# Input laid by groups of tokens, squares added up on VectorE and GpSimd, and a tied order of the first operands, at the head of a one-layer decoder step

## The chip, the core and the metric

The kernel runs on one core of one Trainium2 chip. The metric is the device time of one execution in microseconds (us). The engines are TensorE (PE, its weight loads PEld), VectorE (DVE), ScalarE (ACT), GpSimd (POOL) and SyncE (SP), from whose queue all transfers are issued.

## What is computed

One layer of a hybrid decoder for 1024 prompt tokens and 8 sample tokens, with a model width of 1024. What the change touches is only its first step, the norm and the start of the one wide projection behind it:

```
def _rmsnorm(x, g):
    y = xf * lax.rsqrt(jnp.mean(xf * xf, axis=-1, keepdims=True) + RMS_EPS)
    return (y * g.astype(F32)).astype(x.dtype)
...
xn = _rmsnorm(x, p['norm_mix_g'])
proj = xn @ p['w_in']
pr, pm, pg = ...   # columns for RWKV-7 time mixing, for mLSTM, and for two gates
y_r = RWKV7(pr); y_m = mLSTM(pm)
x = x + (sigmoid(g_r) * (y_r @ r_up) + sigmoid(g_m) * (y_m @ m_up)) @ w_out
x = x + relu(_rmsnorm(x) @ ffn_w1)^2 @ ffn_w2
```

All is in float32.

## The kernel before

**Layout.** The width of 1024 lies in eight slices (k = 0 to 7) of 128 partitions, the tokens lie along the columns. There are 1032 tokens and 8 columns more for the shifted state, in three groups g of 344, 344 and 352 columns (344 of them for the norm). `load_x(g)` loads the eight slices of one group, one transfer each.

**The norm.** `x_rstd(g)` squares the eight slices on ACT (`sq`), and adds them up over slices and partitions with eight float32 matmuls of a matrix of ones into one PSUM bank (`psb`). ACT makes the root's inverse of it with an Ln and an Exp (`rsx`). `x_norm(g)` then works slice by slice: a *mul* on DVE (the gain and `rsx` times `x`, in place), a *hi* on ACT (`xh`, the value rounded to PE's fast float32 format), and a *lo* on DVE (`xl`, what the rounding left).

**The projection.** A weight tile of 128 columns is loaded raw and split in the same way into `whi` (ACT) and `wlo` (DVE). A product takes three matmuls for each slice: `whi` with `xh`, `whi` with `xl`, `wlo` with `xh`. The first two weight tiles (`first_w`) run group by group as soon as operands are there, tile after tile within a group, into banks `psm`. All later tiles run all three groups in turn. 48 matmuls, 24 to a tile, are a token group's work for the first two tiles. `x_last`, the norm of the third group, is called by `emit_jobs` after the first group's products. An evacuation of a product is an ACT copy (`m`) and a DVE instruction that reads the bank (`lw` and `sxg` for the first two tiles).

**What sets the order.** Instructions are recorded one after the other and a scheduler then chooses the order on each engine by its own estimates; each engine works strictly in that order. `tc.issue_after(ins)` ties what is recorded in it behind an instruction. All transfers go through SP's queue in order. Buffers are shared by tags: `v`, `rk`, `ar`, `bk` and `bkt` are later used by the RWKV stage.

**Warming.** `warm(n)` runs n float32 products of `ones` with itself, which nobody reads.

Of the kernel before, what the change touches and what calls it, by code (L numbers as in the profile page):

```python
# [86 lines left out]
def hybrid_step(ctx: ExitStack, tc: tile.TileContext, I: dict, O: dict):  # L87
    nc = tc.nc
    V, S, G, PE = nc.vector, nc.scalar, nc.gpsimd, nc.tensor
    dma = nc.sync.dma_start  # L90
# [3 lines left out]
    wp = ctx.enter_context(tc.tile_pool(name="wp", bufs=2))  # L94
# [7 lines left out]
    ones = cp.tile([128, 128], F32, name="ones")  # L102
    par = cp.tile([128, NPAR], F32, name="par")
    bias = cp.tile([128, 8], F32, name="bias")
    par2 = cp.tile([128, 18], F32, name="par2")
    xo = cp.tile([128, KD, 9], F32, name="xo")
# [18 lines left out]
    def P(name, i=0, rows=slice(0, 128)):  # L125
        c0 = PCOLS[name] + i
        return par[rows, c0 : c0 + 1]
# [7 lines left out]
    def mm(out, lhsT, rhs, start, stop):  # L135
        return PE.matmul(out, lhsT, rhs, start=start, stop=stop)  # L136

    def tt(out, a, b, op):
        V.tensor_tensor(out, a, b, op)  # L139

    def stt(out, a, s, b, op0, op1):
        V.scalar_tensor_tensor(out, a, s, b, op0, op1)  # L142

    def act(out, in_, f, **kw):
        return S.activation(out, in_, f, **kw)  # L145
# [9 lines left out]
    MUL, ADD, SUB, MAX, MIN = ALU.mult, ALU.add, ALU.subtract, ALU.max, ALU.min  # L155
# [7 lines left out]
    def bb():  # L163
        return bank("b", "psb", 3)
# [10 lines left out]
    def gst(name, dt=F32):  # L175
        return gp.tile([128, 346], dt, name=name, tag="gst")

    dma(par[:], I["par"])
    G.memset(ones[:], 1.0)
    log_exp_set()  # L180
    for i, v in enumerate([RMS_EPS, R_GN_EPS, M_GN_EPS, 1.0, 10.0 * math.log(2.0)]):
# [1 line left out]
    B_RMS, B_RGN, B_MGN, B_ONE, B_KK = (bias[:, i : i + 1] for i in range(5))  # L183

    def warm(n):

        pt = bb()
        for i in range(n):
            mm(pt[:, 0:128], ones[:], ones[:], i == 0, i == n - 1)


    def wload(src):
        raw = wp.tile([128, KD, 128], F32, name="wraw", tag="wraw")
        dma(raw[:], src)
        return raw

    def wsplit(raw):
        hi = wp.tile([128, KD, 128], F32R, name="whi", tag="whi")
        lo = wp.tile([128, KD, 128], F32R, name="wlo", tag="wlo")
        act(hi[:], raw[:], AF.Copy)  # L200
        tt(lo[:], raw[:], hi[:].bitcast(F32), SUB)
        return hi, lo
# [32 lines left out]
    def R(shape, name, tag=None, bufs=1, dt=F32):  # L235
        return rp.tile(shape, dt, name=name, tag=tag or name, bufs=bufs)


    xr4 = R([128, 4, NX], "xr4", tag="v")
    xr = [xr4[:, k] for k in range(4)]  # L240
    for k in range(4, KD):
        xr.append(R([128, NX], f"xr{k}", tag=("ar", "bk")[k // 6], bufs=2)[:])

    def load_x(g):
        c0, c1 = RGROUPS[g]
        for k in range(KD):
            dma(xr[k][:, c0:c1], I["xT"][:, k, c0:c1])

    load_x(0)
    first_w = [wload(I["win"][i]) for i in (12, 13)]  # L250
    load_x(1)
    load_x(2)
    dma(con[:], I["con"])
    xa = []
    for k in range(KD):
        xh = xp.tile([128, NX], F32R, name=f"xh{k}", tag=f"x{2 * k}")
        xl = xp.tile([128, NX], F32R, name=f"xl{k}", tag=f"x{2 * k + 1}")
        xa.append((xh, xl))

    rsx = R([128, 3, GN], "rsx", tag="uv", bufs=2)  # L260

    def x_rstd(g):

        c0, c1 = GROUPS[g]
        rs = rsx[:, g]
        pt = bb()
        for k in range(KD):
            sq = gst("sq")[:, :GN]
            act(sq, xr[k][:, c0:c1], AF.Square)
            mm(pt[:, :GN], ones[:], sq, k == 0, k == KD - 1)  # L270
        if g == 0:
            warm(16)
        act(rs, pt[:, :GN], AF.Ln, scale=1.0 / D, bias=B_RMS)
        act(rs, rs, AF.Exp, scale=-0.5)
        dma(d_rs[0:1, c0:c1], rsx[0:1, g])

    def x_norm(g, ks=range(KD)):
        c0, c1 = GROUPS[g]
        for k in ks:
            xh, xl = xa[k]  # L280
            x = xr[k][:, c0:c1]
            stt(x, x, P("g1", k), rsx[:, g], MUL, MUL)
            c2 = RGROUPS[g][1]
            act(xh[:, c0:c2], xr[k][:, c0:c2], AF.Copy)
            tt(xl[:, c0:c2], xr[k][:, c0:c2], xh[:, c0:c2].bitcast(F32), SUB)

    x_rstd(0)
    first_w[0] = wsplit(first_w[0])
    x_norm(0, range(4))
    first_w[1] = wsplit(first_w[1])  # L290
    x_norm(0, range(4, KD))
    x_rstd(1)
    x_norm(1)
    x_rstd(2)

    def x_last():
        x_norm(2)
        for k in range(KD):
            G.tensor_copy(xo[:, k, :], xr[k][:, NT - 9 : NT])
        dma(O["xo"], xo[:])  # L300


# [4 lines left out]
    def evac_shift(dst, ti):  # L307

        mu, omu = P("mu", ti), par2[:, ti : ti + 1]
        carry = {}  # L310

        def f(g, pt):
            c0, c1 = RGROUPS[g]
            n = min(c1, NT) - c0
            m1 = carry.pop(g, None)
            if m1 is None:
                m1 = gst("m1")
                G.memset(m1[:, 0:1], 0.0)
            npr = min(c1, T) - c0
            act(m1[:, 1:npr + 1], pt[:, 0:npr], AF.Copy, scale=mu)  # L320
            if g < 2:
                nx = gst("m1")
                G.tensor_copy(nx[:, 0:1], m1[:, npr:npr + 1])
                carry[g + 1] = nx
            else:
                act(m1[:, npr : npr + NS], pt[:, NT - c0 : NX - c0], AF.Copy, scale=mu)
            stt(dst[:, c0 : c0 + n], pt[:, :n], omu, m1[:, 0:n], MUL, ADD)

        return f
# [125 lines left out]
    def prep(hp):  # L455
# [1199 lines left out]
    order = [0, 4, 1, 5, 2, 6, 3, 7]  # L1655
# [65 lines left out]
    for g, st in enumerate(STEPS):  # L1721
        n = len(st)
# [6 lines left out]
        for u in range(7 * n):  # L1729
            p, j = divmod(u, n)  # L1730
# [3 lines left out]
    n = len(STEPS[3])  # L1734
# [36 lines left out]
    parts = [(0, (0, 1)), (1, (0,)), (1, (1,))]  # L1771
# [144 lines left out]
```

## Time and profile before

| | |
|---|---|
| median of 3 runs | 1664.7 us (1663.85 to 1669.45) |
| the profiled execution | 1665.72 us, its span 1663.9 us |
| busy PE, PEld | 1615.5 us (97%), 1536.9 us (92%) |
| busy DVE, ACT, POOL | 1187.9 us (71%), 758.9 us (46%), 67.2 us (4%) |
| transfers | 200.11 MB, mean 120 GB/s |

The span is the time between the first and the last instruction; the execution's own time is 1.8 us longer. Busy PE is not PE at its peak: matmuls are pipelined, and a recorded matmul lasts longer than the distance to the next one. The speed is read from the distance of starts.

### The profile page before, as it was taken

Reading aid. Unit: us, or ns where it says so; the run is one execution under the profiler, and the core shown is the slowest. Engines: PE = TensorE matmul, PEld = TensorE weight load, DVE = VectorE, ACT = ScalarE, POOL = GpSimd, SP = SyncE. Lnnn points to the kernel's source line nnn. Section 1 sums busy time; section 2 is a strip of 40 time slices with the busy share of each in tenths; the row PEclk is TensorE's granted clock in tenths of the full one; section 3 lists DMA queues with packets and bytes.
Section 4 is the critical chain, followed back from the end, with each engine's and each line's share of the span. In section 5 each row is a group of like instructions: output and inputs, shape, how many; then the busy total and the mean of one; then the engine's idle time right before and its main releaser. Section 6 shows DMA issues by size and latency. Waiting matters only on the chain. (4 is left out here: it accounts for less than half of the span.)

```text
span 1663.9 us, 37007 instructions
## 1 busy us (share of the span) xinstructions
PE 1615.5 (97%) x15338; PEld 1536.9 (92%) x15338; DVE 1187.9 (71%) x2258; ACT 758.9 (46%) x1387; POOL 67.2 (4%) x130
## 2 busy tenths in 40 slices
PE   8999998999999998999999999999999899999997
PEld 7999986888888887899999999999999899999996
DVE  6266658665666597765876798777777787878787
ACT  6466653333332442443544664445555552525324
POOL 1000000000000000000000222000000000000001
PEclk9999999999999999999999999999999999999998
DMA  5133353222211333424743244444434562625212
GB/s 186 52 117 117 106 170 105 65 92 85 81 61 39 127 105 64 108 90 100 255 150 110 97 130 150 148 141 147 147 141 143 176 217 73 208 77 179 90 58 103
DMA packets 111687, 200.11 MB, mean 120 GB/s; under 512 B 18755, under 2 KB 49502, under 8 KB 111006
## 3 DMA queue, kind: packets, MB, share of 16 engines
q1 hardware_dynamic: 111518, 197.73, 37.1%
q8 instruction: 121, 1.98, 0.5%
q14 instruction: 48, 0.39, 0.1%
HBM read 139.73 MB, written 57.95 MB: 119 GB/s over the span
## 5 line engine op out<-in xcount | busy, mean ns | idle before, releaser
L136 PE MATMUL psm<-xh,whi 128*128 128x344 f32 (+2 forms) x1024 | 342.6, 335 | 0.4 <-DVE rkt L142 0.4
L136 PE MATMUL psm<-xh,wlo 128*128 128x344 f32 (+2 forms) x1024 | 332.0, 325 | 0.0
L136 PE MATMUL psm<-xl,whi 128*128 128x344 f32 (+2 forms) x1024 | 331.1, 324 | 0.0
L136 PE MATMUL bank<-hc,wc 128*128 128x258 f32 x2520 | 306.3, 283 | 9.8 <-ACT su L145 4.5
L136 PEld LDWEIGHTS bank<-hc,wc 128*128 128x128 f32 x2520 | 303.9, 190 | 12.2 <-ACT su L145 4.7
L136 PEld LDWEIGHTS psm<-xh,whi 128*128 128x128 f32 (+1 forms) x1024 | 191.5, 187 | 13.3 <-issue 7.7
L136 PEld LDWEIGHTS psm<-xl,whi 128*128 128x128 f32 (+1 forms) x1024 | 191.8, 188 | 4.2 <-issue 1.9
L136 PEld LDWEIGHTS psm<-xh,wlo 128*128 128x128 f32 (+1 forms) x1024 | 191.8, 187 | 2.1 <-issue 0.5
L136 PE MATMUL bank<-cmb,wc 128*128 128x258 f32 x1536 | 189.8, 282 | 0.8 <-ACT s L145 0.5
L136 PEld LDWEIGHTS bank<-cmb,wc 128*128 128x128 f32 x1536 | 186.1, 189 | 1.3 <-ACT s L145 0.7
L136 PE MATMUL bank<-ha,wc 128*128 128x258 f32 x1152 | 143.5, 282 | 0.7 <-DVE u L139 0.4
L136 PEld LDWEIGHTS bank<-ha,wc 128*128 128x128 f32 x1152 | 139.9, 189 | 1.1 <-DVE u L139 0.6
L139 DVE TENSOR_TENSOR wlo<-wraw,whi 128x1024 fp32r<-128x1024 f32 (+1 forms) x65 | 78.7, 1210 | 78.8 <-ACT whi L145 78.8
L145 ACT ACTIVATE wc<-wraw 128x512 fp32r<-128x512 f32 (+1 forms) x109 | 66.2, 612 | 114.6 <-PE bank L136 101.5
L145 ACT ACTIVATE whi<-wraw 128x1024 fp32r<-128x1024 f32 (+1 forms) x65 | 68.1, 1047 | 83.0 <-PE psm L136 54.7
L139 DVE TENSOR_TENSOR xres<-xres,bank 128x516 f32<-128x516 f32 (+1 forms) x136 | 82.8, 656 | 19.1 <-PE bank L136 19.1
L145 ACT ACTIVATE hc<-hl 128x516 fp32r<-128x516 f32 x105 | 65.9, 633 | 57.0 <-DMA hl<-d_h 56.3
L139 DVE TENSOR_TENSOR wc<-wraw,wc 128x512 fp32r<-128x512 f32 (+1 forms) x109 | 72.7, 671 | 20.3 <-ACT wc L145 20.3
L136 PE MATMUL bank<-ha,whi 128*128 128x258 f32 x512 | 82.8, 283 | 0.0
L139 DVE TENSOR_TENSOR hc<-hl,hc 128x516 fp32r<-128x516 f32 x105 | 70.3, 694 | 15.9 <-ACT hc L145 15.7
L139 DVE TENSOR_TENSOR u<-u,bank 128x516 f32<-128x516 f32 (+1 forms) x65 | 44.3, 682 | 37.5 <-PE bank L136 37.3
L136 PEld LDWEIGHTS bank<-ha,whi 128*128 128x128 f32 x512 | 70.7, 189 | 0.1
(385 smaller groups left out, 2619.1 us busy)
## 6 DMA issues: line engine op xcount, KB each, us to landing
hl<-d_h SPq DMA_DIRECT2D x109, 258.0 KB
wraw<-in_win SPq DMA_DIRECT2D x42, 512.0 KB
d_h<-t SPq DMA_DIRECT2D x60, 258.0 KB
a<-in_w SPq DMA_DIRECT2D x45, 256.0 KB
wraw<-in_w SPq DMA_DIRECT2D x18, 512.0 KB
d_gate<-gt SPq DMA_DIRECT2D x48, 172.0 KB
gl<-d_gate SPq DMA_DIRECT2D x32, 258.0 KB
w2r<-in_w SPq DMA_DIRECT2D x16, 512.0 KB
```

The lines of the kernel that those rows point to most:

```text
L136: return PE.matmul(out, lhsT, rhs, start=start, stop=stop)
L139: V.tensor_tensor(out, a, b, op)
L145: return S.activation(out, in_, f, **kw)
```

## The change

`x` is laid by token group instead of by slice: the first group is one tile `x0` that shares the tag `v` (its last four of twelve columns of 344 serve as space for squares, `sqt[0]` and `sqt[1]`), the second lies in two tiles under `rk`, the third in four under `ar` and `bk`. One transfer loads two slices, so 12 take the place of 24, and `par` is issued behind the first group's four instead of at the very start.

Squares are taken two slices at a time (688 columns). For the first group DVE adds them up, and PE has three sums instead of eight; one of the eight slices is squared on DVE. For the second and third group GpSimd adds two pairs each (two instructions of 688 columns), and PE has four sums. Ten warm-up products run at the very start, and eight instead of sixteen behind the first sums.

The *mul*, *hi*, *lo*, the squares of the next group and the splits of the first two weight tiles (now in halves of 512 columns, `whi` and `wlo` in the list) are recorded in an order written out by hand and tied one behind the other on ACT and on DVE (`tied`).

```diff
-    dma(par[:], I["par"])
...
+    x0 = R([128, 12, GN], "x0", tag="v")
+    x1 = [R([128, 4, GN], f"x1{i}", tag="rk", bufs=2) for i in (0, 1)]
+    x2 = [R([128, 2, GN + NS], f"x2{i}", tag=("ar", "bk")[i // 2], bufs=2) for i in range(4)]
...
-        for k in range(KD):
-            dma(xr[k][:, c0:c1], I["xT"][:, k, c0:c1])
+        for k in range(0, KD, 2):
+            dma(xin[g][k // 2], I["xT"][:, k : k + 2, c0:c1])

     load_x(0)
+    dma(par[:], I["par"])
     first_w = [wload(I["win"][i]) for i in (12, 13)]
...
+    sqt = [x0[:, 8:10], x0[:, 10:12], *[R([128, 2, GN], "sq2", tag="bkt", bufs=2)[:] for i in (0, 1)]]
+    def tied(e, f):
+        if e in chains:
+            with tc.issue_after(chains[e].ins):
+                chains[e] = f()
+        else:
+            chains[e] = f()
+        return chains[e]
+    def square(g, j):
+        return act(sqt[j], xin[g][j][:, :, 0:GN], AF.Square)
...
     def x_rstd(g):
+        if g == 0:
+            tt(sqt[0][:, 0], sqt[0][:, 0], sqt[0][:, 1], ADD)
+            parts = [sqt[0][:, 0], sqt[3][:, 0], sqt[3][:, 1]]
+        else:
+            for j in (1, 2):
+                G.tensor_tensor(sqt[0], sqt[0], sqt[j], ADD)
+            parts = [sqt[i][:, j] for i in (0, 3) for j in (0, 1)]
+        for i, sq in enumerate(parts):
+            mm(pt[:, :GN], ones[:], sq, i == 0, i == len(parts) - 1)
+        if g == 0:
+            warm(8)
+        tied("a", lambda: act(rs, pt[:, :GN], AF.Ln, scale=1.0 / D, bias=B_RMS))
+        tied("a", lambda: act(rs, rs, AF.Exp, scale=-0.5))
-        for k in range(KD):
-            sq = gst("sq")[:, :GN]
-            act(sq, xr[k][:, c0:c1], AF.Square)
-            mm(pt[:, :GN], ones[:], sq, k == 0, k == KD - 1)
-        if g == 0:
-            warm(16)
...
+    warm(10)
+    for j in range(3):
+        square(0, j)
+        if j:
+            tt(sqt[0], sqt[0], sqt[j], ADD)
+    act(sqt[3][:, 0], xr(0, 6), AF.Square)
+    tt(sqt[3][:, 1], xr(0, 7), xr(0, 7), MUL)
...
     x_rstd(0)
-    first_w[0] = wsplit(first_w[0])
-    x_norm(0, range(4))
-    first_w[1] = wsplit(first_w[1])
-    x_norm(0, range(4, KD))
+    run("mul.0.0 whi.0.0 hi.0.0 mul.0.1 wlo.0.0 hi.0.1 lo.0.0 mul.0.2 whi.0.1 hi.0.2 lo.0.1 wlo.0.1 mul.0.3 sq.1.0 hi.0.3 lo.0.2 "
...
     x_rstd(1)
-    x_norm(1)
+    run("mul.1.0 sq.2.0 hi.1.0 mul.1.1 hi.1.1 lo.1.0 mul.1.2 sq.2.1 hi.1.2 lo.1.1 mul.1.3 sq.2.2 hi.1.3 lo.1.2 mul.1.4 sq.2.3 "
...
     x_rstd(2)
```

In a list entry the first number is the token group (for `whi` and `wlo` the weight tile) and the second the slice, the pair of slices or the half.

On PE the program before begins as follows: eight sums for the first group, sixteen warm-up products, then sums for the second group among the first products (`psb` are banks of sums, `psm` of products).

```order
L136 MATMUL psb_156<-sq_175,ones_76 128x344
L136 MATMUL psb_156<-sq_178,ones_76 128x344
L136 MATMUL psb_181<-ones_76 128x128 x16
L136 MATMUL psb_233<-sq_234,ones_76 128x344
L136 MATMUL psb_233<-sq_237,ones_76 128x344
L136 MATMUL psm_338<-xh0_139,whi_201 128x344
L136 MATMUL psm_338<-xl0_140,whi_201 128x344
L136 MATMUL psm_338<-xh0_139,wlo_202 128x344
L136 MATMUL psb_233<-sq_240,ones_76 128x344
```

With the change PE begins with ten warm-up products and three sums, and the sums of the second group stand behind products of slice 5 of the first weight tile (`psm_296`) and slice 2 of the second (`psm_327`).

```order
L136 MATMUL psb_148<-ones_76 128x128 x10
L136 MATMUL psb_170<-x0_104,ones_76 128x344
L136 MATMUL psb_170<-sq2_147,ones_76 128x344 x2
L136 MATMUL psb_175<-ones_76 128x128 x8
L136 MATMUL psm_296<-xh0_129,whi_166 128x344
...
L136 MATMUL psm_296<-xh5_139,whi_166 128x344
L136 MATMUL psm_327<-xh2_133,wlo_169 128x344
L136 MATMUL psb_223<-x0_104,ones_76 128x344 x2
L136 MATMUL psb_223<-sq2_147,ones_76 128x344 x2
L136 MATMUL psm_296<-xl5_140,whi_166 128x344
```

So the sums of the second group moved from ahead of the first products to behind 25 of them, and two tiles' products now alternate.

On DVE the first group's work stands so before, behind the split of the first weight tile (`xr` are the input tiles, a SCALAR_TENSOR_TENSOR with `rsx` is a *mul*, an `xl` a *lo*):

```order
L139 TENSOR_TENSOR wlo_202<-wraw_118,whi_201 128x1024
L142 SCALAR_TENSOR_TENSOR xr4_105<-xr4_105,par_77,rsx_155 128x344 x3
L139 TENSOR_TENSOR xl0_140<-xr4_105,xh0_139 128x344
L139 TENSOR_TENSOR xl1_142<-xr4_105,xh1_141 128x344
L139 TENSOR_TENSOR xl2_144<-xr4_105,xh2_143 128x344
L142 SCALAR_TENSOR_TENSOR xr4_105<-xr4_105,par_77,rsx_155 128x344
L139 TENSOR_TENSOR wlo_218<-wraw_120,whi_217 128x1024
```

And with the change, where the adds of squares stand ahead of it (`x0_104` is the first group's tile with the space for squares):

```order
L139 TENSOR_TENSOR x0_104<-x0_104 128x688
L139 TENSOR_TENSOR x0_104<-x0_104,sq2_146 128x688
L139 TENSOR_TENSOR sq2_147<-x0_104 128x344
L139 TENSOR_TENSOR x0_104<-x0_104 128x344
...
L142 SCALAR_TENSOR_TENSOR x0_104<-x0_104,par_77,rsx_145 128x344 x2
L139 TENSOR_TENSOR wlo_167<-wraw_116,whi_166 128x512
L139 TENSOR_TENSOR xl0_130<-x0_104,xh0_129 128x344
L142 SCALAR_TENSOR_TENSOR x0_104<-x0_104,par_77,rsx_145 128x344
L139 TENSOR_TENSOR xl1_132<-x0_104,xh1_131 128x344
L139 TENSOR_TENSOR wlo_167<-wraw_116,whi_166 128x512
```

DVE gained four instructions at the head, a *mul* comes first instead of a whole split, and splits come in halves between a *mul* and a *lo*.

On GpSimd, which so far had only fills and small copies here, the adds for the second and third group are new, the first behind an instruction (ISA) that changes the engine's configuration:

```order
L291 ISA
L291 TENSOR_TENSOR x0_104<-x0_104 128x688
L291 TENSOR_TENSOR x0_104<-x0_104,sq2_146 128x688
L383 COPY m1_324<-m1_321 128x1
L378 MEMSET m1_352 128x1
L291 TENSOR_TENSOR x0_104<-x0_104 128x688
```

Before, that instruction stood ahead of the first add of a much later stage (L1394).

## Rows read from the trace of the kernel before

**Rows 1.** Windows of the head: busy time (and instructions) of each engine, granted clock, DMA.

```profile
12.00:27.30 15.30, 15.30 (x78) 11.27 (x76) 13.27 (x26) 14.79 (x36) 0.10 (x1) 1.00 0.75 252
27.30:48.50 21.20, 21.20 (x135) 21.19 (x134) 15.00 (x31) 12.52 (x24) 5.72 (x14) 1.00 0.17 46
```

**Rows 2.** Timeline of PE: start, duration, instruction and count.

```profile
4.54 7.87 PE L136 MATMUL psb<-sq,ones 128*128 128x344 f32 x16 [4.54 <-ACT sq L145]
...
16.75 0.58 PE L136 MATMUL psm<-xh,whi 128*128 128x344 f32 x1
...
17.68 4.89 PE L136 MATMUL psb<-sq,ones 128*128 128x344 f32 x16
...
27.47 0.32 PE L136 MATMUL psm<-xh,whi 128*128 128x344 f32 x1
...
40.71 0.33 PE L136 MATMUL psm<-xh,whi 128*128 128x352 f32 x1
...
48.49 0.32 PE L136 MATMUL psm<-xh,whi 128*128 128x344 f32 x1
```

**Rows 3.** Timeline of DVE, from its first split to the last `xl`.

```profile
14.03 1.23 DVE L139 TENSOR_TENSOR wlo<-wraw,whi 128x1024 fp32r<-128x1024 f32 x1 [11.21 <-ACT whi L145]
...
22.28 0.58 DVE L142 SCALAR_TENSOR_TENSOR xr<-xr,par,rsx 128x344 f32<-128x344 f32 x1
...
23.19 0.57 DVE L142 SCALAR_TENSOR_TENSOR xr<-xr,par,rsx 128x344 f32<-128x344 f32 x1
...
39.15 0.96 DVE L139 TENSOR_TENSOR xl<-xr,xh 128x352 fp32r<-128x352 f32 x2
```

**Rows 4.** Timeline of ACT, from the first square to the first Exp.

```profile
3.90 0.94 ACT L145 ACTIVATE sq<-xr 128x344 f32<-128x344 f32 x2 [1.89 <-DMA xr<-in_xT]
...
8.68 0.49 ACT L145 ACTIVATE sq<-xr 128x344 f32<-128x344 f32 x1 [0.32 <-DMA xr<-in_xT]
12.51 0.55 ACT L145 ACTIVATE rsx<-psb,bias 128x344 f32<-128x344 f32 x1 [3.34 <-PE psb L136]
12.95 1.05 ACT L145 ACTIVATE whi<-wraw 128x1024 fp32r<-128x1024 f32 x1
13.90 0.48 ACT L145 ACTIVATE rsx<-rsx 128x344 f32<-128x344 f32 x1
```

**Rows 5.** Timeline of PE's weight loads in the first sums, one for each pass.

```profile
5.82 0.34 PEld L136 LDWEIGHTS psb<-sq,ones 128*128 128x128 f32 x1 [0.24 <-issue]
6.39 0.34 PEld L136 LDWEIGHTS psb<-sq,ones 128*128 128x128 f32 x1 [0.23 <-issue]
...
10.41 1.45 PEld L136 LDWEIGHTS psb<-sq,ones 128*128 128x128 f32 x5 [0.24 <-issue]
```

**Rows 6.** Timeline of SP's queue: the first issues of transfers.

```profile
0.74 0.41 SPq L178 DMA_DIRECT2D par<-in_par  x1
1.20 3.74 SPq L247 DMA_DIRECT2D xr<-in_xT  x8
```

**Rows 7.** Groups by shape: count, then total us, mean ns, and idle time before.

```profile
L145 ACT ACTIVATE sq<-xr 128x344 f32<-128x344 f32 x24 | 10.7, 480 | 3.3 <-DMA xr<-in_xT 3.1
L145 ACT ACTIVATE wc<-wraw 128x512 fp32r<-128x512 f32 x101 | 63.3, 628 | 104.8 <-PE bank L136 91.7 <-issue 6.5 <-DVE wraw L139 4.1
L139 DVE TENSOR_TENSOR acc<-acc,sq 128x516 f32<-128x516 f32 x21 | 14.5, 691 | 1.6 <-ACT sq L145 1.3
L139 DVE TENSOR_TENSOR wlo<-wraw,whi 128x1024 fp32r<-128x1024 f32 x64 | 78.2, 1222 | 78.8 <-ACT whi L145 78.8
```

**Rows 8.** Timeline of DVE and GpSimd where both add at once, much later.

```profile
967.84 5.54 DVE L1427 TENSOR_TENSOR xres<-xres,acc 128x516 f32<-128x516 f32 x4
967.88 6.54 POOL L1427 TENSOR_TENSOR xres<-xres,acc 128x516 f32<-128x516 f32 x4 [5.32 <-DVE acc L139]
```

**Rows 9.** The configuration instruction's line on GpSimd: ns least/median/most, starts, wait behind.

```profile
L1394 POOLq MODIFY_POOL_CONFIG  x2: 11/11/11, 737.4 to 737.4; - x2
...
  DVE acc L139: 165.0, 1
```

More of the change, by code (lines that the diff above doesn't have):

```diff
@@ L138, in tt @@
     def tt(out, a, b, op):
-        V.tensor_tensor(out, a, b, op)
+        return V.tensor_tensor(out, a, b, op)
     def stt(out, a, s, b, op0, op1):
-        V.scalar_tensor_tensor(out, a, s, b, op0, op1)
+        return V.scalar_tensor_tensor(out, a, s, b, op0, op1)
     def act(out, in_, f, **kw):
@@ L236, in R, with xr @@
         return rp.tile(shape, dt, name=name, tag=tag or name, bufs=bufs)
[L239 to L242, printed above, removed]
+    x0 = R([128, 12, GN], "x0", tag="v")
+    x1 = [R([128, 4, GN], f"x1{i}", tag="rk", bufs=2) for i in (0, 1)]
+    x2 = [R([128, 2, GN + NS], f"x2{i}", tag=("ar", "bk")[i // 2], bufs=2) for i in range(4)]
+    xin = [[x0[:, k : k + 2] for k in range(0, KD, 2)], [x[:, k : k + 2] for x in x1 for k in (0, 2)], [x[:] for x in x2]]
+    def xr(g, k, n=GN):
+        return xin[g][k // 2][:, k % 2, 0:n]
     def load_x(g):
         c0, c1 = RGROUPS[g]
-        for k in range(KD):
-            dma(xr[k][:, c0:c1], I["xT"][:, k, c0:c1])
+        for k in range(0, KD, 2):
+            dma(xin[g][k // 2], I["xT"][:, k : k + 2, c0:c1])
     load_x(0)
+    dma(par[:], I["par"])
     first_w = [wload(I["win"][i]) for i in (12, 13)]
@@ L260, in hybrid_step @@
     rsx = R([128, 3, GN], "rsx", tag="uv", bufs=2)
+    sqt = [x0[:, 8:10], x0[:, 10:12], *[R([128, 2, GN], "sq2", tag="bkt", bufs=2)[:] for i in (0, 1)]]
+    chains = {}
+    def tied(e, f):
[7 more added lines that the diff above has]
+        return act(sqt[j], xin[g][j][:, :, 0:GN], AF.Square)
     def x_rstd(g):
@@ L266, in x_rstd @@
         pt = bb()
-        for k in range(KD):
-            sq = gst("sq")[:, :GN]
-            act(sq, xr[k][:, c0:c1], AF.Square)
-            mm(pt[:, :GN], ones[:], sq, k == 0, k == KD - 1)
-        if g == 0:
-            warm(16)
[L273 to L285, printed above, removed]
@@ L287, in hybrid_step @@
-    x_rstd(0)
-    first_w[0] = wsplit(first_w[0])
-    x_norm(0, range(4))
-    first_w[1] = wsplit(first_w[1])
-    x_norm(0, range(4, KD))
-    x_rstd(1)
-    x_norm(1)
-    x_rstd(2)
+        if g == 0:
[5 more added lines that the diff above has]
+            parts = [sqt[i][:, j] for i in (0, 3) for j in (0, 1)]
@@ new lines, in x_rstd, with x_mul, x_hi @@
+        for i, sq in enumerate(parts):
[4 more added lines that the diff above has]
+        tied("a", lambda: act(rs, rs, AF.Exp, scale=-0.5))
+        dma(d_rs[0:1, c0:c1], rsx[0:1, g])
+    def x_mul(g, k):
+        return stt(xr(g, k), xr(g, k), P("g1", k), rsx[:, g], MUL, MUL)
+    def x_hi(g, k):
+        c0, c1 = RGROUPS[g]
+        return act(xa[k][0][:, c0:c1], xr(g, k, c1 - c0), AF.Copy)
@@ new lines, in x_lo, with run @@
+    def x_lo(g, k):
+        c0, c1 = RGROUPS[g]
+        return tt(xa[k][1][:, c0:c1], xr(g, k, c1 - c0), xa[k][0][:, c0:c1].bitcast(F32), SUB)
+    def run(order):
+        for x in order.split():
+            f, *n = x.split(".")
+            i, j = (int(c) for c in n)
+            if f == "mul":
+                tied("d", lambda: x_mul(i, j))
+            elif f == "hi":
+                tied("a", lambda: x_hi(i, j))
+            elif f == "lo":
+                tied("d", lambda: x_lo(i, j))
+            elif f == "sq":
+                tied("a", lambda: square(i, j))
+            else:
+                hi, lo, raw = [w[:, 4 * j : 4 * j + 4] for w in (first_w[i][0], first_w[i][1], raws1[i])]
+                if f == "whi":
+                    tied("a", lambda: act(hi, raw, AF.Copy))
+                else:
+                    tied("d", lambda: tt(lo, raw, hi.bitcast(F32), SUB))
@@ new lines, in hybrid_step @@
+    warm(10)
[5 more added lines that the diff above has]
+    tt(sqt[3][:, 1], xr(0, 7), xr(0, 7), MUL)
+    raws1 = first_w
+    first_w = [[wp.tile([128, KD, 128], F32R, name=nm, tag=nm) for nm in ("whi", "wlo")] for _ in raws1]
+    x_rstd(0)
+    run("mul.0.0 whi.0.0 hi.0.0 mul.0.1 wlo.0.0 hi.0.1 lo.0.0 mul.0.2 whi.0.1 hi.0.2 lo.0.1 wlo.0.1 mul.0.3 sq.1.0 hi.0.3 lo.0.2 "
+        "mul.0.4 whi.1.0 sq.1.1 hi.0.4 lo.0.3 mul.0.5 wlo.1.0 whi.1.1 sq.1.2 hi.0.5 lo.0.4 mul.0.6 sq.1.3 hi.0.6 lo.0.5 wlo.1.1 "
+        "mul.0.7 hi.0.7 lo.0.6 lo.0.7")
@@ L296, in x_last, with x_norm @@
+    x_rstd(1)
+    run("mul.1.0 sq.2.0 hi.1.0 mul.1.1 hi.1.1 lo.1.0 mul.1.2 sq.2.1 hi.1.2 lo.1.1 mul.1.3 sq.2.2 hi.1.3 lo.1.2 mul.1.4 sq.2.3 "
+        "hi.1.4 lo.1.3 mul.1.5 hi.1.5 lo.1.4 mul.1.6 hi.1.6 lo.1.5 mul.1.7 hi.1.7 lo.1.6 lo.1.7")
+    x_rstd(2)
+    def x_norm(g):
+        for k in range(KD):
+            x_mul(g, k)
+            x_hi(g, k)
+            x_lo(g, k)
     def x_last():
@@ L298, in x_last @@
         for k in range(KD):
-            G.tensor_copy(xo[:, k, :], xr[k][:, NT - 9 : NT])
+            G.tensor_copy(xo[:, k, :], xr(2, k)[:, GN - 9 : GN])
         dma(O["xo"], xo[:])
```

## The prediction

> **What bounds the kernel now.** I read the table of windows first, since the change touches only the first 50 us. Between 27.30 and 48.50 us PE works the whole 21.20 us, with 135 matmuls in it, and DVE 15.00; between 12.00 and 27.30 PE counts as busy too, but with 78 matmuls for 15.30 us [rows 1]. So the timeline of PE comes next: 16 matmul passes with `ones` (two passes to one float32 product) fill 4.54 to 12.4, 16 more stand from 17.68 to 22.6 between products of the projection, and only from 27.3 on do the projection's matmuls follow each other without a break: 84 of them from 27.47 to 40.71, 0.158 us each, then 48 of 352 columns at 0.162, until the next tile's first stands at 48.49 [rows 2]. After that the program is the same on all five engines but for a few neighbours that change places, and PE keeps waiting for the same things. So I judge the change by one number: when the 48th matmul of the third token group ends, now 48.5 us. What is won or lost there I carry unchanged to the end.
>
> PE is the limit from 27.3 on, but DVE is close behind it. It starts at 14.03, never rests, and ends its last `xl` of the group stage at 40.1; a `mul` and a `lo` together take 0.913 us (22.28 to 23.19) [rows 3]. PE takes that last `xl` some 4 us later, as the 24 matmuls of the first weight tile before it take that long. That cover is what the change uses up.
>
> **The start, part by part.** ACT's timeline gives the first chain now: the first square starts at 3.90 and the last at 8.68, both on DMA; the Ln starts at 12.51 when the sums are done; a 1.05 us split of weights goes ahead of the Exp, which ends at 14.38 [rows 4]. PE is late there: one weight load, so one pass, every 0.57 us up to 10.41, then five in 1.45, 0.29 each [rows 5]. These are the lower and the upper of its two levels (1.2 and 2.4 GHz), although the granted clock reads 1.00 all along.
>
> In the new order `x` is first in SP's queue, 0.46 us earlier (1.20 against 0.74), and half as many issues carry the same bytes (eight take 3.74 us now) [rows 6]. The last piece would land between 6.4 (all of the issuing saved: 8.68 - 0.46 - 1.87) and 8.4. The first and the last square lie 4.8 us apart against 3.74 for the issues, so the transfer sets more of it than the issue: I take 7.9. The pair before it lands 1.3 earlier, at 6.6. Its square of 688 columns takes 0.78 (0.48 at 344, 0.63 at 512), the second add of 688 on DVE 0.87 (0.69 at 516, 1.22 at 1024) [rows 7]: done at 8.3. Behind it on DVE stand the square of the eighth slice and the halves' add, 0.45 each (half of the 0.913 of a pair): PE can start at 9.2. Three sums instead of eight are six passes, 1.7 us at the upper level, 3.4 at the lower. I take the upper, since ten warm-up products run as soon as `ones` is filled; the lower stays in the range, because PE then rests some 4 us before the sums. Ln 0.55, Exp 0.48, hand-overs 0.2, no split between: DVE starts its first `mul` at 12.2 (13.9 at the lower level) where its first split now starts at 14.03.
>
> The Trainium skill, "TensorE: Matmul & The Clock Gate" (What's actually happening), says that the clock starts at 1.2 GHz, that activity raises it, and that idleness takes it back. The rise at 10.41 agrees. By it the rest ahead of the sums would give away what the warm-up bought, and the sum below would end 1.7 us higher.
>
> **DVE's work.** From its first `mul` to the last `lo` it has 24 pairs (24 x 0.913 = 21.9 us), four half splits of 512 columns (0.6 each, 2.4) and four evacuations from PSUM (counted as half a pair each, 1.8). None of this is new but its order. 12.2 + 26.1 = 38.3.
>
> **GpSimd's adds.** New are four adds of 688 columns, two for each of the second and third token groups. At 967.84 DVE and GpSimd do four adds of 516 columns side by side: DVE needs 5.54 us for four that take 0.69 each elsewhere, GpSimd 6.54 [rows 7, 8]. They take turns: every `xres` of DVE after the first waits about (5.54 - 0.70)/3 - 0.60 = 1.0 us for GpSimd. Both operands of these instructions lie in SBUF, as with `mul` and `lo`. Scaled to 688 columns that is 1.35 us an add. From below, nothing, if the adds fall where DVE waits anyway; from above the whole turn, 6.54/4 x 688/516 = 2.18. I take 1.35, the same pair of engines in the same situation: 4 x 1.35 = 5.4 us on DVE, the engine that has no rest.
>
> The Trainium skill, "SBUF — State Buffer" (SBUF: two separate sides), speaks against the change here: GpSimd and a DVE instruction with two SBUF inputs share a port that is locked for a whole instruction, and the loser blocks fully. The turns in the rows agree. By the rule a `mul` that meets an add at its start pays the add's whole length, so the rule leans to the upper end of the bounds just given, and the sum below would be some 1668 to 1670 us.
>
> Before the first add stands an instruction that changes GpSimd's configuration. It now stands at 737.4, takes 11 ns and is followed by 165.0 us of waiting for something else [rows 9], so its true cost doesn't show. In the new order it has cover from about 2 to 18 us, where the first add is due. I cost it at nothing.
>
> **Waits that DVE gets.** Squares, splits and `hi` share ACT in a tied order. In the first group ACT has 8 `hi`, 4 half splits and 4 squares of 688, about 3.3 + 2.2 + 2.8 = 8.3 us, for DVE's 9.7, and a `lo` late in the group waits for a `hi` behind a square: 0.9. The second group's sums need the third square (some 19.7), two adds in turns with DVE (22), four sums on PE (2.3), Ln and Exp (1.2 with hand-overs): 25.7 to 26.2, while DVE is through with the first group at 12.2 + 9.7 + 0.9 + 2.7 = 25.5. It waits 0.2 to 0.7; I take 0.6. For the third group the four sums stand in PE's queue behind twelve products of the second group and wait for its `lo`s; I take 0.9. Behind them the start of the third group waits 0.3 for its first `hi`. Together 2.7 us (none to 5).
>
> **The sum.** 38.3 + 5.4 + 2.7 = 46.4 for the start of the last `lo`. PE has fewer sums (11 against 24) and starts the projection near 13.4 instead of 16.75, but it now runs at DVE's pace to the end, and 26 matmuls are left behind the last `lo`: 26 x 0.162 = 4.2, with the hand-over 4.3. That makes 50.7 against 48.5: 2.2 us later. The profiled execution took 1665.7 us, 1.0 more than the median of 1664.7; with 2.2 added it is 1667.9, and by the median 1666.9.
>
> **The rivals.**
> - The change does what its parts suggest and DVE isn't held: no turns, no waits. 38.3 + 4.3 = 42.6, 5.9 earlier, 1658.8. For it: PE needs only 13.4 + 144 x 0.159 + 8 x 0.58 = 41 us for its own work. Against it: four adds that by the rows hold DVE, and two Exps on the way. Chance 0.08.
> - GpSimd's adds fall half into DVE's waits, or the last piece lands at 6.9: 2.5 to 3.5 us less than my sum, 1663.8. Chance 0.20.
> - The sums run at the lower level: +1.7, 1668.6. For it the slow passes of [rows 5]; against it the warm-up. The rule of the Trainium skill's "TensorE: Matmul & The Clock Gate" given above is this case. Chance 0.22.
> - The other side: a turn of GpSimd costs the full 2.18 us or more. Each add stands twice on the path, in DVE's turn and in the chain to the next Exp, but DVE's wait for that Exp is partly the same time; four times 0.83 gives +3.3, 54.0 us, 1670.2. From 2.1 us a turn on this is slower by over 0.3%. A late configuration would add to it. Chance 0.14.
> - As summed: 0.36, with 1664.5 to 1669.5 as its own range.
>
> **How the numbers follow.** 0.3% of 1664.7 is 5 us, about what a measurement here can tell from no change. Faster by more takes nearly the whole first rival and some luck: 0.10. Slower by more takes the last rival or the lower level with some of it: 0.16. Within: 0.74. The likeliest is 1666.9. With all bounds at once the time would lie between 1656 and 1675; 1660.0 to 1672.0 leaves out most of the first rival and the end of the last.
>
> **What would show it.** The first `mul` on DVE at 11 to 14 us; `mul` and `lo` of 1.3 us or more beside the adds of 688; DVE busy up to 45 to 47 with short waits for Exp; PE with gaps between projection matmuls until then, and the last 352-column matmul ending at 49 to 52. I am wrong if the adds leave DVE's durations as they are, if the first add comes long after its squares, or if the time differs after 50 us by more than at 50 us.

## The result

The changed kernel takes 1678.45 us in the median of six runs (1672.46 to 1680.6) against 1664.66 us before (1661.62 to 1669.45), a ratio of 1.0070 with an interval of 1.0052 to 1.0088. Timed a second time it gave 1.0068 (1.0045 to 1.0091). By the ratios that is 11 to 12 us slower, by the two medians 13.8; I had forecast 1666.9 us, and the result lies above my range. The profiled execution took 1680.6 us, its span is 1678.8 us.

The head is the program up to the next tile's first matmul, behind the third group's 48. Its windows in the changed kernel, with the columns of [rows 1] (us, then PE, PEld, DVE, ACT and POOL busy, the granted clock, the DMA share, GB/s):

```profile
0.00:12.00 12.00, 7.91 (x26) 6.42 (x27) 3.03 (x7) 4.10 (x5) 1.35 (x16) 0.87 0.86 304
12.00:27.30 15.30, 11.08 (x56) 8.21 (x55) 12.76 (x20) 10.57 (x22) 4.39 (x2) 0.99 0.66 231
27.30:48.50 21.20, 14.97 (x80) 13.07 (x79) 19.50 (x36) 12.99 (x27) 11.12 (x16) 0.95 0.10 27
48.50:70.00 21.50, 21.50 (x123) 21.50 (x122) 4.58 (x6) 11.21 (x14) 0.41 (x3) 0.89 0.14 50
```

In the third stretch PE, which worked all of it before, is busy 14.97 us of 21.20, with 80 matmuls for 135, and DVE 19.50 for 15.00. And the granted clock, 1.00 in both stretches of [rows 1], is under 1.00 in all four.

The timeline of PE in the changed kernel, which answers to [rows 2] (start, duration, instruction, count, idle time before and its releaser):

```profile
0.99 4.57 PE L136 MATMUL psb<-ones 128*128 128x128 f32 x20 [0.99 <-POOL bias L181]
8.66 1.43 PE L136 MATMUL psb<-x,ones 128*128 128x344 f32 x2 [3.10 <-DVE x L139]
9.89 2.47 PE L136 MATMUL psb<-sq,ones 128*128 128x344 f32 x4
12.18 1.96 PE L136 MATMUL psb<-ones 128*128 128x128 f32 x16
...
33.21 0.43 PE L136 MATMUL psm<-xh,whi 128*128 128x344 f32 x1 [1.59 <-DVE sxg L142]
...
47.11 0.63 PE L136 MATMUL psm<-xh,whi 128*128 128x352 f32 x1 [3.80 <-ACT xh L145]
47.54 0.49 PE L136 MATMUL psm<-xl,whi 128*128 128x352 f32 x1
47.84 0.49 PE L136 MATMUL psm<-xh,wlo 128*128 128x352 f32 x1
...
53.30 0.32 PE L136 MATMUL psm<-xh,whi 128*128 128x352 f32 x1
53.46 0.33 PE L136 MATMUL psm<-xl,whi 128*128 128x352 f32 x1
...
57.67 0.32 PE L136 MATMUL psm<-xh,whi 128*128 128x344 f32 x1
```

The next tile's first matmul starts at 57.67 us, 9.18 later than in [rows 2]. Three pieces make that up. PE is ready for the third group at 43.31 (47.11 less the 3.80 that it stood), 2.60 later than before. Then it stands, that is, it is idle, for 3.80 us. Then the 48 matmuls take 10.56 us for 7.78, 2.78 more: they start 0.293 us apart up to 53.3, and 0.162 apart, as before, from there on. 2.60 + 3.80 + 2.78 = 9.18.

The timeline of DVE in the changed kernel, which answers to [rows 3]:

```profile
13.56 1.06 DVE L142 SCALAR_TENSOR_TENSOR x<-x,par,rsx 128x344 f32<-128x344 f32 x2 [4.80 <-ACT rsx L145]
...
20.44 1.99 DVE L142 SCALAR_TENSOR_TENSOR x<-x,par,rsx 128x344 f32<-128x344 f32 x1
22.35 1.95 DVE L139 TENSOR_TENSOR xl<-x,xh 128x344 fp32r<-128x344 f32 x1
...
27.70 1.07 DVE L142 SCALAR_TENSOR_TENSOR x<-x,par,rsx 128x344 f32<-128x344 f32 x2 [1.25 <-ACT rsx L145]
...
30.71 1.96 DVE L142 SCALAR_TENSOR_TENSOR x<-x,par,rsx 128x344 f32<-128x344 f32 x1
32.59 0.56 DVE L142 SCALAR_TENSOR_TENSOR sxg<-psm,par,m 128x344 f32<-128x344 f32 x1
33.08 1.62 DVE L139 TENSOR_TENSOR xl<-x,xh 128x344 fp32r<-128x344 f32 x1
...
39.45 2.04 DVE L142 SCALAR_TENSOR_TENSOR x<-x,par,rsx 128x344 f32<-128x344 f32 x4 [0.45 <-ACT rsx L145]
...
45.91 0.57 DVE L142 SCALAR_TENSOR_TENSOR x<-x,par,rsx 128x344 f32<-128x344 f32 x1
46.40 0.56 DVE L142 SCALAR_TENSOR_TENSOR lw<-psm,par,m 128x344 f32<-128x344 f32 x1
46.89 0.56 DVE L142 SCALAR_TENSOR_TENSOR sxg<-psm,par,m 128x344 f32<-128x344 f32 x1
47.37 0.51 DVE L139 TENSOR_TENSOR xl<-x,xh 128x352 fp32r<-128x352 f32 x1
```

The timeline of GpSimd in the changed kernel, its four adds of squares:

```profile
19.45 2.60 POOL L291 TENSOR_TENSOR x<-x 128x688 f32<-128x688 f32 x1 [17.57 <-ACT x L145]
22.13 1.79 POOL L291 TENSOR_TENSOR x<-x,sq 128x688 f32<-128x688 f32 x1
...
30.28 2.02 POOL L291 TENSOR_TENSOR x<-x 128x688 f32<-128x688 f32 x1 [1.23 <-ACT x L145]
...
32.67 1.65 POOL L291 TENSOR_TENSOR x<-x,sq 128x688 f32<-128x688 f32 x1
```

Beside each add one *mul* or *lo* of DVE takes 1.62 to 1.99 us instead of 0.57 or 0.51. The four together lose 1.42 + 1.44 + 1.39 + 1.11 = 5.36 us.

Why PE stands from 43.31 to 47.11 is the main reading. The view names ACT's `xh` as releaser. The timeline of ACT in the changed kernel shows that the `xh` of the third group's first four slices had long been done (at 42.14; the one that ends at 47.02, behind 46.52, is the eighth slice's, which the first matmul doesn't read):

```profile
7.14 0.49 ACT L145 ACTIVATE sq<-x 128x344 f32<-128x344 f32 x1 [0.29 <-DMA x<-in_xT]
12.46 0.55 ACT L145 ACTIVATE rsx<-psb,bias 128x344 f32<-128x344 f32 x1 [4.83 <-PE psb L136]
...
40.49 1.65 ACT L145 ACTIVATE xh<-x 128x352 fp32r<-128x352 f32 x4
```

What ends just ahead of 47.11 is DVE's `lw` (46.40, done at 46.96). It reads the bank of the second group's first product. There are two `psm` banks (`bank("mm", "psm", 2)`), and the third group's first product takes that one again. Such a wait for a bank stands in the timeline of PE once under its own name: at 33.21 the second group's product for the second weight tile has stood 1.59 us for `sxg` (32.59, done at 33.15), which frees the other bank. `lw` stands on DVE behind the eighth *mul* of the third group, here as before. The timeline of DVE in the kernel before has it at

```profile
38.66 0.57 DVE L142 SCALAR_TENSOR_TENSOR lw<-psm,par,m 128x344 f32<-128x344 f32 x1
```

and so done at 39.2, ahead of PE's need at 40.71 [rows 2]; it cost nothing.

### The profile page after: what moved, and what is told of

Its sections match the earlier page's. It is cut to its first block, busy times and chain, and to the rows that moved or that the text cites. A ratio compares the mean times of both kernels' runs of the same rounds, so it can differ in the third digit from the quotient of the medians.

```text
span 1678.8 us, 36950 instructions
## 1 busy us (share of the span) xinstructions
PE 1621.4 (97%) x15316; PEld 1542.5 (92%) x15316; DVE 1196.8 (71%) x2264; ACT 759.0 (45%) x1377; POOL 76.5 (5%) x134
## 5 line engine op out<-in xcount | busy, mean ns | idle before, releaser
L139 DVE TENSOR_TENSOR wlo<-wraw,whi 128x1024 fp32r<-128x1024 f32 (+2 forms) x67 | 78.9, 1178 | 70.7 <-ACT whi L145 70.6
L145 ACT ACTIVATE whi<-wraw 128x1024 fp32r<-128x1024 f32 (+2 forms) x67 | 68.4, 1021 | 85.8 <-PE psm L136 58.4
```

Of the source, the lines that this page charges most:

```text
L139: return V.tensor_tensor(out, a, b, op)
```

## The experiments

The theory that I set out to test: (A) PE's stand is the wait for the bank that `lw` frees, and `lw` is late because DVE is; (G) DVE is late because of GpSimd's adds; and the lower clock level behind the stand, and in the first sums, costs the rest. Rivals: the layout and its buffers cost the time; the order by hand does; or (E) later stages lose clock because everything is shifted.

The table gives for each kernel the start of the next tile's first matmul (48.49 in [rows 2]) and the loss against the kernel before that its ratio stands for (the ratio less one, times 1666 us). The start comes from one profile of each kernel, and between two profiles of the kernel before it moved by 1.7 us, so differences of that size between two rows show nothing by themselves.

| kernel | next tile's first, us | against 48.49 | loss by the ratio, us (interval) |
|---|---|---|---|
| changed | 57.67 | +9.2 | 11.7 (8.7 to 14.7) |
| changed, again | 59.59 | +11.1 | 11.3 (7.5 to 15.2) |
| free bank | 51.76 | +3.3 | 5.5 (2.8 to 8.2) |
| filled stand | 56.37 | +7.9 | 6.5 (4.3 to 8.7) |
| all sums on PE | 49.71 | +1.2 | 0.3 (-1.7 to 2.3) |
| kernel before, shifted | 55.94 | +7.5 | 8.2 (5.5 to 10.7) |
| free bank, sums on PE | 48.95 | +0.5 | 2.2 (0.5 to 3.8) |
| the same, longer warm-up | 47.39 | -1.1 | -2.3 (-4.2 to -0.5) |
| untied | 52.20 | +3.7 | 6.3 (4.2 to 8.5) |
| layout alone | 47.97 | -0.5 | -0.3 (-1.8 to 1.2) |
| longer warm-up alone | 56.68 | +8.2 | 6.8 (4.2 to 9.5) |
| before, again | 46.81 | -1.7 | one run |

**Other banks for the third group.** The third group's products of the first two weight tiles go to banks of `psb`; everything else is as in the changed kernel.

```diff
-        def part(w, g):
+        def part(w, g, early=True):
...
-            pt = bmain()
+            pt = bb() if early and g == 2 else bmain()
...
-                part(w, g)
+                part(w, g, False)
```

> The third token group's two products of the first weight tiles go to banks of psb instead of psm, so they need no bank that DVE's lw and sxg of the second group must first empty; DVE's order stays the same. Theory A (PE stands 3.8 us because the bank is freed only by lw at 46.4 us, behind seven muls on DVE; ACT's xh, which the profile names, had long been done): PE goes on at once at about 43.3 us, is paced by DVE's lo to about 47.9, and the last 352-column matmul ends 26 matmuls later, at about 52 instead of 57.7; no rise of matmul spacing to 0.29 us. Median some 5 us below the changed kernel. Rival B (PE waits for operands of the third group): it still stands until about 47 us and the end stays within 1 us of 57.7.

The timeline of PE in this kernel, the third group's first matmul and the next tile's:

```profile
43.86 0.33 PE L136 MATMUL psb<-xh,whi 128*128 128x352 f32 x1
...
51.76 0.32 PE L136 MATMUL psm<-xh,whi 128*128 128x344 f32 x1
```

And its DVE:

```profile
47.11 0.57 DVE L142 SCALAR_TENSOR_TENSOR lw<-psm,par,m 128x344 f32<-128x344 f32 x1
...
48.08 0.52 DVE L139 TENSOR_TENSOR xl<-x,xh 128x352 fp32r<-128x352 f32 x1
```

DVE is 0.7 us later than in the changed kernel, `lw` included, and PE no longer cares: no stand, and the 48 matmuls take 7.90 us. Behind the start of the last `lo` are left 51.76 - 48.08 = 3.7 us of matmuls, about 23, where I had forecast 26. The ratio is 1.0033 (1.0017 to 1.0049). The bank is shown to be the wait. The lower level is gone with the stand; the next run keeps the wait and takes the idleness away.

**PE kept at work while it stands.** 16 warm-up products (32 passes) ahead of the third group.

```diff
+                if g == 2:
+                    with tc.issue_after(last_mm[0].ins):
+                        warm(16)
```

> Sixteen products of ones (read by nobody) are put into PE's queue between the second and the third token group, where PE stood 3.8 us; the wait for the bank stays. Theory A (the stand lets PE fall to its lower level, which costs 22 matmuls at 0.293 instead of 0.162 us, 2.9 us): the third group still starts at about 47.1 but runs at 0.162 from its first matmul and ends at about 54.9. Rival C (the lower level comes from the slack work between 12 and 43 us, not from the stand): spacing of 0.29 us stays for the first 6 us and the end stays at 57 to 58.

The timeline of PE in this kernel:

```profile
44.84 3.73 PE L136 MATMUL psb<-ones 128*128 128x128 f32 x32
48.52 0.40 PE L136 MATMUL psm<-xh,whi 128*128 128x352 f32 x1
```

The third group then takes 56.37 - 48.52 = 7.85 us against 10.56: the clock's part of the loss is 2.7 us. DVE ran 1.4 us later in this execution (`lw` at 47.80, done at 48.37), so the head gains 1.3 of it and ends at 56.37 where I had expected 54.9. With both runs the lower level is shown to follow from the stand. The ratio is 1.0039 (1.0026 to 1.0052).

**No adds on GpSimd.** All eight squares of the second and third group go to PE.

```diff
-            for j in (1, 2):
-                G.tensor_tensor(sqt[0], sqt[0], sqt[j], ADD)
-            parts = [sqt[i][:, j] for i in (0, 3) for j in (0, 1)]
+            parts = [sqt[i][:, j] for i in range(4) for j in (0, 1)]
```

> GpSimd's four adds are left out; PE sums eight squares instead of four for the second and third group (8 x 0.58 us more on PE), all else as changed. Theory A (the adds hold DVE 1.35 us each): no mul or lo above 0.6 us, DVE saves about 5.4 us of holding but waits up to 2.4 us more for each Exp, lw comes 1 to 5 us earlier (42 to 45 us), and the end follows it: lw + 0.6 + 7.8 us plus what the clock costs, 51 to 56. Rival D (DVE's pace is set by ACT's tied order, not by the adds): lw stays at 46 us or later.

No single *mul* or *lo* takes more than 0.57 us any more, the last `lo` starts at 41.63 (5.74 earlier), `lw` at 41.15, and PE's stand shrinks:

```profile
41.86 0.40 PE L136 MATMUL psm<-xh,whi 128*128 128x352 f32 x1 [0.65 <-ACT m L145]
```

It is the same bank (`lw` is done at 41.72, while the last `xh` ended at 41.33), but 0.65 us and no loss of clock behind it: the 48 matmuls take 7.85 us. In all the profiles with a stand here (the changed kernel twice, this one, the untied kernel and the longer warm-up alone) PE goes on 0.14 or 0.15 us behind the end of `lw`. The ratio is 1.0002 (0.9990 to 1.0014): with the adds gone from GpSimd, the change costs nothing that these runs can tell.

**The kernel before, made later by warm-up products alone.**

```diff
-            warm(16)
+            warm(56)
```

> The kernel before with 56 instead of 16 warm-up products behind the first sums, 40 x 0.233 = 9.3 us of PE work that nothing needs, so that its first 50 us end about 9.3 us later and nothing else differs. Theory E (the 5 us by which the changed profile loses more than its head did come from a lower clock in later stages, which the shift or the run decides and not the changed head): the time grows by 9 to 14 us, and a profile may show low granted clock in 250 to 300 us as the changed one does. Rival F (later loss comes from the changed layout or tags): it grows by 9.3 us and no more, with the stages after 50 us as long as before.

The head ends 7.5 us later, where I had expected 9.3 (1.0 of the difference is that the first 16 passes took 6.89 us in this execution for 7.87), and the ratio stands for 8.2 (5.5 to 10.7): a shift is carried to the end. Between 245 and 276 us the loss grew by a further 4 us. I took that for (E), a shift that brings on a stretch of the lower level; the kernel before, profiled again (below), shows it without any shift, and that reading fell.

**Both causes out: a free bank and all sums on PE.** The diffs of the first and third experiment together.

> The changed kernel with two edits together: the third group's first product takes a psb bank, and all eight squares go to TensorE with no add on GpSimd. Theory A+G (two things made the head late: the bank that `lw` frees, and DVE's slowing under the GpSimd adds): PE starts the third group right behind the second, the last `lo` starts at 41.6 to 42.5 us, the next tile's first product at 46 to 47.5 us (48.49 in the kernel before), and the stages behind it come 1 to 2.5 us earlier than before up to 245 us; the median is 0 to 3 us below that of the kernel before. Rival (the eight extra matmuls of the sums push the products so far that PE's own work sets the end): the third group starts at 41 us or later with no stand, and the next tile's first product is at 48.5 to 50.

Here I expected too much. The last `lo` starts at 41.75 as forecast, but the third group starts at 41.17 and the next tile at 48.95: the rival holds, PE's own work now sets the end. It begins the projection at 15.02 instead of 16.75, but from 12.00 to 27.30 it is busy only 13.95 us of 15.30. The ratio is 1.0013 (1.0003 to 1.0023).

**The same with a longer warm-up,** so that PE rests less ahead of the first sums.

```diff
-    warm(10)
+    warm(18)
```

> As the kernel with free bank and no GpSimd adds, and with the 10 matmuls of the warm-up ahead of the first sums made 18, so that PE does not rest between them and the first sums. Theory (the sums run at the lower level because PE rested some 3 us ahead of them): the three sums have the granted clock's upper level, the first `mul` starts at 12.0 to 12.6 us, 1.2 to 1.7 earlier than in the changed kernel, and the next tile's first product comes as much earlier than without the longer warm-up. Rival (the level is lower at the sums whatever stands ahead of them, so early in the program): the sums have the lower level and the first `mul` stays at 13.5 to 13.8, or later by what the longer warm-up takes from the sums.

The timeline of PE in this kernel:

```profile
0.99 5.73 PE L136 MATMUL psb<-ones 128*128 128x128 f32 x36 [0.99 <-POOL bias L181]
9.11 0.84 PE L136 MATMUL psb<-x,ones 128*128 128x344 f32 x2 [2.38 <-DVE x L139]
9.79 1.32 PE L136 MATMUL psb<-sq,ones 128*128 128x344 f32 x4
...
39.62 0.32 PE L136 MATMUL psb<-xh,whi 128*128 128x352 f32 x1
...
47.39 0.32 PE L136 MATMUL psm<-xh,whi 128*128 128x344 f32 x1
```

The three sums end 2.0 us behind their start (9.11 to 11.11); in the changed kernel it was 3.7 (8.66 to 12.36). The first *mul* starts at 12.31 for 13.87, and the head ends 1.56 us earlier than without the longer warm-up, 1.10 earlier than in [rows 2], though not than in the second profile of the kernel before (46.81). The ratio is 0.9986 (0.9975 to 0.9997): the one version whose interval lies below the kernel before, by little.

**Untied.** `tied` only calls its function, and the scheduler orders ACT and DVE.

```diff
-        if e in chains:
-            with tc.issue_after(chains[e].ins):
-                chains[e] = f()
-        else:
-            chains[e] = f()
-        return chains[e]
+        return f()
```

> The changed kernel with the tying taken away: the scheduler orders the instructions of ScalarE and VectorE. Theory (the tied order costs nothing by itself: the evacuation `lw` stands behind the third group's `mul` either way): PE stands for 3 to 5 us at the third group, the next tile's first product is at 56.5 to 59 us, and the median is within 2 us of the changed kernel's. Rival (the tied order is what puts `lw` late): PE's stand is under 1.5 us and the next tile's first product is at 52 to 54 us.

The timeline of PE in this kernel:

```profile
21.69 2.66 PE L136 MATMUL psb<-x,ones 128*128 128x344 f32 x4 [2.11 <-POOL x L286]
...
36.32 0.40 PE L136 MATMUL psm<-xh,whi 128*128 128x344 f32 x1 [1.91 <-DVE lw L142]
...
44.36 0.40 PE L136 MATMUL psm<-xh,whi 128*128 128x352 f32 x1 [0.23 <-ACT xh L145]
```

The rival holds: `lw` of the second group stands at 43.64 instead of 46.40, PE stands 0.23 us for it, and the third group's matmuls keep the upper level (7.84 us). The first group's `lw` (35.61) is late in its turn and costs a stand of 1.91, and the first *mul* starts at 14.93. Against the changed kernel the order by hand is worth 5.5 us of the head in the wrong direction. The ratio is 1.0038 (1.0025 to 1.0051).

**The layout alone.** The kernel before with x by groups, 12 transfers, and `par` behind the first four; squares, sums and order stay.

```diff
-    dma(par[:], I["par"])
...
+    x0 = R([128, 12, GN], "x0", tag="v")
+    x1 = [R([128, 4, GN], f"x1{i}", tag="rk", bufs=2) for i in (0, 1)]
+    x2 = [R([128, 2, GN + NS], f"x2{i}", tag=("ar", "bk")[i // 2], bufs=2) for i in range(4)]
...
+        for k in range(0, KD, 2):
+            dma(xin[g][k // 2], I["xT"][:, k : k + 2, c0:c1])
...
+    dma(par[:], I["par"])
```

> The kernel before with the new layout alone: x in tiles by group, 12 transfers of two rows' pairs each, the parameters behind the first group; squares, sums and order as before. Theory (the layout moves the landing by about 1 us and nothing else): the next tile's first product is 0 to 1.5 us earlier or later than 48.49, no stand of PE over 1 us at the third group, and the median within 2 us of the kernel before. Rival (the layout itself, its buffers taken from later stages' tags, costs the time): the head ends within 1.5 us of before but the stages behind 245 us come 3 us or more later.

The head ends 0.52 us earlier, the ratio is 0.9998 (0.9989 to 1.0007). The profiled execution was 3.6 us late at 276, but the kernel before, profiled again, was 2.2 late there too. The layout costs nothing that these runs can tell.

**Both kernels profiled again, unchanged.**

> The kernel before, unchanged, profiled once more. Theory (the stretches of the lower clock behind 245 us differ from one execution of the same program to the next): its head ends within 0.3 us of the first profile's (next tile's first product at 48.49 us), but the stages at 276, 655 or 700 us stand 1 us or more off those of the first profile. Rival (those stretches belong to the program): all stages stand within 0.5 us of the first profile's.

> The changed kernel, unchanged, profiled and timed once more. Theory as for the kernel before, profiled again: the head's loss repeats (next tile's first product at 56.5 to 58.5 us, PE's stand 3 to 4.5 us), while the further 3 us between 245 and 310 us and the step near 655 us don't repeat within 1 us. Rival: the offsets of the first profile (+9.2, +12.1, +13.0) repeat within 0.5 us. The median is 1672 to 1680 either way.

The windows from 245 to 310 us, in the kernel before, first profile:

```profile
245.00:310.00 65.00, 57.75 (x1138) 49.89 (x1136) 45.91 (x121) 23.22 (x47) 0.96 (x1) 1.00 0.33 104
```

in the changed kernel:

```profile
245.00:310.00 65.00, 58.88 (x895) 49.30 (x895) 46.07 (x115) 21.11 (x42) 0.96 (x1) 0.92 0.38 122
```

in the changed kernel again:

```profile
245.00:310.00 65.00, 58.08 (x944) 48.13 (x946) 47.28 (x117) 22.33 (x44) 0.96 (x1) 1.00 0.41 128
```

and in the kernel before again:

```profile
245.00:310.00 65.00, 58.00 (x1096) 49.90 (x1096) 43.96 (x118) 21.43 (x45) 0.96 (x1) 0.92 0.30 95
```

The same program has a granted clock of 0.92 there in one execution and 1.00 in the other, both ways round. By ACT's splits of the same weights, the kernel before fell from 1.6 us ahead of its first profile at 245 to 2.5 behind at 306, was 0.4 behind at 757 and 0.9 ahead at 1616. Against the same first profile, the changed kernel went from 9.1 behind at 245 to 13.0 behind at 757 the first time and from 11.3 to 7.2 the second time. So from 245 to 757 us the two executions of the kernel before differ by 2.0 us (4.1 up to 306), and those of the changed kernel by 8.0. The head's loss repeats in kind: ready 4.79 later, a stand of 3.52, 2.79 of clock, 11.10 in all. It ends later than I expected (59.59 for 56.5 to 58.5); the last transfer alone landed 1.0 us later. The row of its stand:

```profile
49.02 0.63 PE L136 MATMUL psm<-xh,whi 128*128 128x352 f32 x1 [3.52 <-ACT xh L145]
```

My expectation for the head of the kernel before was wrong: it moves too, by 1.7 us, as its first 16 passes took 6.25 us instead of 7.87.

**The longer warm-up alone,** in the changed kernel.

> The changed kernel with the 10 matmuls of the warm-up ahead of the first sums made 18, and nothing else. Theory (the first sums ran at the lower level because PE rested ahead of them; the bank that `lw` frees still sets the third group's start): the sums have the upper level, the first `mul` starts at 12.0 to 12.6 us, DVE is 1.2 to 1.7 us earlier throughout, PE still stands 3 to 4.5 us at the third group and falls to the lower level there, and the next tile's first product is at 55.5 to 57 us (57.67 without). Rival (the head's loss follows from the late sums): PE's stand goes below 2 us and the next tile's first product is below 54 us.

The first *mul* starts at 12.80 (I had expected 12.6 at the latest), PE stands 3.52 all the same, and the head ends at 56.68: the lost bank doesn't follow from the late sums. DVE didn't stay ahead as I had expected: `lw` is at 46.75. Part of the third group's sums ran at the lower level this time, as this row of PE shows, against 1.32 in the changed kernel for the same four passes:

```profile
34.74 2.38 PE L136 MATMUL psb<-x,ones 128*128 128x344 f32 x4
```

and DVE waited 1.17 us for the Exp behind them instead of 0.45. The ratio is 1.0041 (1.0025 to 1.0057).

## Why the prediction was wrong

- **The landing and the squares** were right. The last transfer was there at 7.1 us (8.1 in the second profile; I took 7.9), PE began the sums at 8.66 (9.76; 9.2).
- **The first sums at the upper level** were wrong, my rival with a chance of 0.22 was right. They took 3.70 us for 1.7, and the first *mul* came at 13.56 (14.77) instead of 12.2. PE had rested 3.10 us between the warm-up and the sums, and the granted clock from 9 to 12 us was 0.50; in the second profile, where PE was idle from 4.86 to 9.76, it was 1.00 up to 7 us, 0.65 from 7 to 8 and 0.50 from 8 to 13, so it fell while PE rested. "TensorE: Matmul & The Clock Gate" of the Trainium skill (What's actually happening), by which idleness takes the clock back, agrees. The ten warm-up products hardly reached the upper level before that: their 20 passes took 4.57 us (3.87 in the second profile), 0.23 each, against 0.12 for the 16 behind the sums, though the granted clock reads 1.00 over them. The longer warm-up kept the upper level; it both worked longer and left a shorter rest, and no run parts the two. I had the rule and set it aside.
- **DVE's work, GpSimd's adds and the waits** were right. From the first *mul* to the last `lo` I summed 34.2 us, and it took 33.81; the adds cost 5.36 for 5.4, the waits for Exp 1.25 and 0.45 for 0.6 and 0.9. The turn was the 1.35 us of [rows 7, 8], not GpSimd's full add. The lock that "SBUF — State Buffer" (SBUF: two separate sides) of the Trainium skill describes shows in whole instructions held, but only one of DVE's for each add: the `sxg` at 32.59, with one operand in PSUM, took its 0.56 us while GpSimd's last add ran, and the *lo* behind it took 1.62.
- **"26 matmuls are left behind the last `lo`" was the step that failed.** All 48 were left, 10.3 us for 4.3. I counted operands and forgot the bank: the third group can't begin before `lw`, which stands on DVE just ahead of the last `lo`. In [rows 2, 3] PE's need stood at 40.71 and DVE's last `lo` ended at 40.1, so the evacuation ahead of it, done at 39.2, was covered by 1.5 us; DVE's delay of 7.7 us (46.40 for 38.66) used that up while PE's own delay was 2.6. 22 more matmuls are 3.6 us, and the lower level behind the stand 2.8; less the 0.3 by which the 48 began ahead of that `lo`, this is the 6.0 by which the term fell short. The first *mul* came 1.4 late, DVE's work took 0.4 less than summed, and so the head came 7.0 later than my 50.7. With the banks free the term is 3.7 us, near my 4.3.
- **The order by hand** I had taken for neutral in this place. It isn't: untied, `lw` comes 2.8 us earlier. Part of it can be read off: `lw` stands there behind six *lo* of the third group instead of seven (0.4 us), and DVE's *mul* lost 4.2 us to the adds instead of 5.36, as one add ran while DVE waited 1.60 us anyway. The rest is not taken apart.
- **"Carried unchanged to the end"** held within what can be told: the head's 9.2 to 11.1 against 11.3 to 11.7 by the ratios, and in the table only the untied kernel has an interval that lies clearly above its head's loss (it begins at 4.2, the head lost 3.7). The further 4 to 6 us of the first profile after 245 us are those of one execution; the second gained 4 back. Why the granted clock is lower there in some executions and not in others stays open.

## What to carry to other kernels

A matmul needs its operands and its bank: in counting what is left behind the last operand, ask for each product which instruction frees the bank, on which engine it stands, and what is queued ahead of it. "Perfetto Trace Analysis" of the Trainium skill (Matmuls) asks for rotation through banks so that evacuation and the next group overlap; two banks gave that while DVE was ahead and lost it when DVE came 7.7 us later and PE only 2.6, and other banks for the third group's two products brought 5.9 of 9.2 us back. An edit that slows the engine that evacuates can be paid for on PE twice, as it was here, with a stand and with clock behind it, and what it saved on PE (11 sums instead of 24) brought nothing while PE stood for DVE.

## What was not expected of the hardware

A stand of 3.5 to 3.8 us costs PE a second time: about 20 matmuls at 0.293 instead of 0.162 us in both profiles of the changed kernel, about 9 in the kernel with the longer warm-up alone, while stands of 0.23 and 0.65 us cost none. In between it went either way: the stand of 1.59 us at 33.21 was followed by a granted clock of 1.00 in the first profile, but in the second profile one of 1.58 there was followed by 0.50 from 35 to 38 us, and in the untied kernel the stand of 2.11 by 0.50 from 22 to 25 (four passes in 2.66 us). Ten warm-up products with a rest of 3.10 us behind them kept nothing for the sums, eighteen with a rest of 1.87 or 2.38 did. And a program on one core, unchanged, differs between executions by 1.7 us in its first 50 us (the kernel before, through its slow first passes) and by 4 us from 245 to 306 us (the same) or 8 from 245 to 757 (the changed kernel). In the windows where they part the granted clock differs: 1.00 and 0.92 from 245 to 310, and in the changed kernel also 0.83 and 0.96 from 650 to 690; that the clock is the whole of it is not shown.
